# A decoder trunk on one core: the third place for a weight sum, and a held load

## The chip, the cores and the metric

The kernel runs on one core of a Trainium2 chip. The metric is the device time of one execution in microseconds; the time before is the median of three runs.

The engines are TensorE (PE: matmuls, and PEld for the loads of their stationary operand), VectorE (DVE), ScalarE (ACT), GpSimd (POOL) and SyncE (SP). Each runs its own list of instructions in order and waits on semaphores for the others. SP, ACT and POOL also issue DMA transfers; an issue stands in its engine's list like any instruction.

## The reference

Two layers, each of a mixing sublayer and a SwiGLU feed-forward sublayer, with a residual and a layer norm behind each. x is 512 tokens by 1024 channels in float32. The mixing sublayer starts with one projection of x, cut into the operands of two branches, attention and retention:

```python
z = jnp.einsum('bsd,dc->bsc', x, w_in) + b_in
q_a, k_a, v_a, q_r, k_r, v_r, g_r, gate_a, gate_b = jnp.split(z, SPLIT_POINTS, axis=-1)
for gi, (window, dilation) in enumerate(ATTN_GROUPS):      # (128, 1), (512, 4), (2048, 16)
    o, lse = _dilated_window_attention(q_a[:, :, gi], k_a[:, :, gi], v_a[:, :, gi], bias, window, dilation)
    ...
wts = jax.nn.softmax(jnp.stack(lses, axis=0), axis=0)
y_a = jnp.sum(wts[..., None] * jnp.stack(outs, axis=0), axis=0)
y_r = _retention(q_r, k_r, v_r)                            # 4 heads, chunkwise
merged = sigmoid(gate_a) * (y_a @ w_attn_proj) + sigmoid(gate_b) * (silu(g_r) * y_r) @ w_ret_proj
x = layer_norm(ALPHA * x + merged @ w_out);  x = layer_norm(ALPHA * x + swiglu(x))
```

Attention has six heads of width 64 in each of three groups. Query t of a group looks at the keys t, t - d, ..., t - window, with a bias by distance. The groups' outputs are added with weights that come from the softmax denominators.

## The kernel before

**Precision.** Every float32 matmul is three matmuls: each operand is split into a high part (a cast on ScalarE, `whi`, `xh`) and a low part (a subtraction on VectorE, `wlo`, `xl`), and high by high, high by low and low by high are added up in PSUM.

**Products.** Most projections are done with seven half-size products in place of eight (a Strassen-Winograd scheme). The weights of such a group are four blocks B11, B12, B21 and B22 and sums of them: P1 = B11 + B12, P2 = P1 + B22, P3 = B12 + B22, P4 = P2 + B21. Sums of x (`xs`) are made once per layer. The products are numbered 1 to 7 and add up in three PSUM accumulators A, X and C: products 1, 6, 7 and 4 in A, 2 in X, 5 and 3 in C. `ORDER` lists them with their operands, and two other orders are cut from it:

```python
ORDER = ((1, "A11", "B11"), (2, "A12", "B21"), (5, "S1", "P1"), (3, "S4", "B22"),
         (6, "S2", "P2"), (7, "S3", "P3"), (4, "A22", "P4"))
WIDE = tuple(ORDER[i] for i in (0, 2, 4, 1, 5, 3, 6))     # products 1, 5, 6, 2, 7, 3, 4
WIDE1 = tuple(ORDER[i] for i in (0, 1, 2, 4, 3, 5, 6))    # products 1, 2, 5, 6, 3, 7, 4
```

`wide` runs a group on TensorE: per product, 2 column halves by 4 slices of the contraction by 3 matmuls. After each product `ev` reads its accumulator (L810 a copy on ScalarE, L812, L815 and L818 sums on VectorE), and the next product in the same accumulator waits for that reading. `Right` makes the weight operands: it loads blocks into `raw` buffers (a pool of eight, each 128 x 1024), makes the sums on VectorE (L374 for P1 and P3, L378 for P2 and P4), and the high and low parts (L356 on ScalarE, L362 on VectorE).

**The attention stage**, once per layer. First come projections of q and k for the first pair of heads, then of v (two groups of `tall`, whose sums at the end are L505 and L508, and which write v to memory). Then, for the second and third pair of heads, comes a third-order projection of q and k (L233, L95, L783) followed by `qk_group`, one group of `wide` for both other orders. These are four groups of `qk_group` in all, two per layer. While TensorE works on a pair's projections, the blocks of the pair before run as side work, cut into small steps: `scores` (two small matmuls per block into `px`, then L572 on VectorE and the exponentials L574 on ScalarE), `turn` (transposes L583 on TensorE, and the copy L584 into `sT`), `values` (matmuls of `sT` with v, and the copy L595). Behind a pair's blocks comes a tail that weighs the two orders of groups: it writes their maxima and denominators to memory (L609) and reads them back in another arrangement (L612 into `mb`), works out the weights (L618 to L628), writes the second order's weights (L627, `wb` to `exd2`), reads them back rearranged (L631 into `fa`), and then expands, transposes and applies them (L638 on POOL, L644 on TensorE, L649 to L653). The tails of the first two pairs run beside the next pair's blocks, the third beside the first retention head.

**What sets the order.** The code gives instructions in one order, and a scheduler reorders each engine's list by its own estimate of when operands are ready. So where an instruction stands in an engine's list is seen in the built program, not in the code. Once built, each engine's order is fixed. L609, L612, L627 and L631 are all issued on ScalarE.

Of the kernel before, what the change touches and what calls it, by code (L numbers as in the profile page):

```python
# [15 lines left out]
ALU = mybir.AluOpType  # L16
# [3 lines left out]
P = 128  # L20
# [3 lines left out]
NI = S // P  # L24
# [30 lines left out]
def hybrid_kernel(ctx, tc, x, rel_bias, w_in, b_in, w_attn_proj, w_ret_proj, w_out,  # L55
# [3 lines left out]
    pe, act, dve, pool = nc.tensor, nc.scalar, nc.vector, nc.gpsimd  # L59
# [25 lines left out]
    def mm3(ps, ah, al, bh, bl, start, stop):  # L85
        mm(ps, ah, bh, start, False)
        mm(ps, ah, bl, False, False)
        mm(ps, al, bh, False, stop)

    def psum(name="px"):  # L90
        return psm.tile([P, S], F32, tag="mm", name=name)
# [5 lines left out]
    def raw(name="raw"):  # L97
        return rawp.tile([P, 1024], F32, tag="raw", name=name)

    def work(name):  # L100
        return wk.tile([P, S], F32, tag="w2", name=name)
# [4 lines left out]
    def view(t, a, b):  # L106
        return t[:, :a * b].rearrange("p (a b) -> p a b", a=a)

    def load(src, a, b):
        v = view(raw(), a, b)  # L110
        for v_, s_ in pieces(v, src):
            nc.sync.dma_start(v_, s_)
        return v
# [211 lines left out]
    WIDE = tuple(ORDER[i] for i in (0, 2, 4, 1, 5, 3, 6))  # L325
    WIDE1 = tuple(ORDER[i] for i in (0, 1, 2, 4, 3, 5, 6))

    class Right:
# [8 lines left out]
        def load(self, *names):  # L337
            for n in names:
                if (n, 0) in self.t:
                    continue  # L340
                for u, (a, b) in enumerate(self.shapes):
                    if n == "P1" and not self.adds:
                        self.t[n, u] = view(raw(), a, b)
                        continue
                    r = self.t[n, u] = load(self.src({"P1": "B11", "P3": "B12"}.get(n, n), u), a, b)
                    if n in ("P1", "P3"):
                        pool.dma_start(r, self.src({"P1": "B12", "P3": "B22"}[n], u), accum_op=ALU.add)  # L347
# [18 lines left out]
        def begin(self, n):  # L366

            if n == "B11":
                self.load(*self.loads)
            elif n in ("P1", "P3") and not self.adds:  # L370
                for u in range(len(self.shapes)):
                    if n == "P3":
                        self.t[n, u] = self.t["B12", u]
                    dve.tensor_tensor(out=self.t[n, u], in0=self.t["B12", u], in1=self.t["B11" if n == "P1" else "B22", u], op=ALU.add)  # L374
            elif n in ("P2", "P4"):
                for u in range(len(self.shapes)):
                    r = self.t["P1", u]
                    dve.tensor_tensor(out=r, in0=r, in1=self.t["B22" if n == "P2" else "B21", u], op=ALU.add)  # L378
            return self.high(n)
# [57 lines left out]
    def wide(right, left, ev):  # L437


        ps = {}  # L440
        for (i, an, bn), ((h, l),) in zip(right.order, right.operands()):
            c = CHAIN[i]
            if i in FIRST:
                ps[c] = psum("ps")
            for q in range(2):
                cs = slice(q * P, (q + 1) * P)
                for k in range(4):
                    ah, al = left(an, k, slice(0, 256))
                    mm3(ps[c][:, q * 256:(q + 1) * 256], h[:, k, cs], l[:, k, cs], ah, al,
                        i in FIRST and q == 0 and k == 0, k == 3)  # L450
                    tick(STEP / 2)
            ev(i, ps[c])
# [91 lines left out]
    def toeplitz(h, off, n):  # L544
        return bass.AP(tensor=bflat.tensor, offset=bflat.offset + h * (L0 + 2 * L1) + off + P - 1,
                       ap=[[HPG * (L0 + 2 * L1) - 1, P], [1, n]])

    def attention_pair(hp, qk, v, yp, bias, yaT):


# [26 lines left out]
        def turn(i, od):  # L577
            pxs, s, j0 = wrk[i, od]
            sT = wk.tile([P, 2, 2 * P], F32, tag="w2", name="sT")
            px = pxs[0].rearrange("p (h c) -> p h c", h=2)  # L580
            for hh in range(2):
                for j in range(j0, 2):
                    pe.transpose(px[:, hh, j * P:(j + 1) * P], s[:, hh, j * P:(j + 1) * P], ident)  # L583
            act.copy(out=sT[:, :, j0 * P:], in_=px[:, :, j0 * P:])  # L584
            wrk[i, od] = (pxs, sT, j0)

        def values(i, od):
# [9 lines left out]
        fa = sm.tile([P, 2, NI, 2], F32, tag="fa", name="fa", bufs=2)  # L597
# [30 lines left out]
            dve.tensor_tensor(out=fa[:, 0], in0=ea[:, 0], in1=wa, op=ALU.mult)  # L628

        def weighed():  # L630
            act.dma_start(fa[:, 1], exd2.rearrange("(l r) c -> l r c", r=4))  # L631

        wide_, weights = {}, {}
# [52 lines left out]
    def layer(ly, cp):  # L686
# [80 lines left out]
        with stage("attn") as ap_, stage("attw", 4) as aw:  # L767
# [17 lines left out]
            def qk_group(hp):  # L785

                def src(b, u):
                    k = 4 if b[1] == "2" else 0
                    c = (C_KA if b[2] == "2" else C_QA) + hp * P
                    return w_l[:, k:k + 4, c:c + 2 * GW].rearrange("p k (g c) -> p k g c", g=2)[:, :, :, :P]  # L790

                sn = {}

                def put(v, j, half):
                    for g in range(2):
                        bs = (bQs[ly], bT)[j]
                        c = (0, C_KA // P)[j] + (g * GW + hp * P) // P
                        o_, i_ = qk[hp, g][:, j], v[:, g]
                        if g:
                            o_ = o_.rearrange("p (r l) -> p r l", r=4)[:, :, half * 64:half * 64 + 64]  # L800
                            i_ = i_.rearrange("p (l r) -> p r l", r=4)
                        else:
                            o_ = o_[:, half * 256:half * 256 + 256]
                        act.activation(out=o_, in_=i_, func=AF.Identity, bias=bs[:, c:c + 1], scale=(HD ** -0.5, 1.0)[j])

                def ev(i, ps):
                    p2 = ps.rearrange("p (q t) -> p q t", q=2)
                    if i in (1, 5, 6):
                        sn[i] = view(work("sn"), 2, 256)
                        act.copy(out=sn[i], in_=p2)  # L810
                    elif i == 2:
                        dve.tensor_tensor(out=sn[1], in0=p2, in1=sn[1], op=ALU.add)  # L812
                        put(sn[1], 0, 0)
                    elif i == 3:
                        dve.tensor_tensor(out=sn[6], in0=p2, in1=sn[6], op=ALU.subtract)  # L815
                        put(sn[6], 1, 0)
                    elif i == 7:
                        dve.tensor_tensor(out=sn[5], in0=sn[5], in1=p2, op=ALU.subtract)  # L818
                        put(sn[5], 1, 1)
                    elif i == 4:  # L820
                        put(p2, 0, 1)

                wide(Right(src, [(4, 256)], WIDE, ("B11", "B12", "P1", "B22", "B21"), False), x_left, ev)

            if ly == 0:
                x0 = [slot("x0", F32) for _ in range(NI)]
# [154 lines left out]
            n = [nothing]  # L981
# [8 lines left out]
        with stage("ret") as rp:  # L990
# [139 lines left out]
            for dp in range(KD // 2):  # L1130
                h, l = was[dp]
# [239 lines left out]
```

## Time and profile before

| | |
|---|---|
| median of 3 runs | 2170.4 us (2165.8 to 2170.66) |
| the profiled execution | 2161.78 us, its span 2160.0 us |
| TensorE busy | 2134.5 us of the span |
| VectorE, ScalarE busy | 1475.8 us, 1046.5 us |
| data moved by DMA | 351.30 MB, 163 GB/s mean |

The profile shows one execution. A row of a timeline gives the start in us from the span's start, the length, the engine, the line of the kernel, the operation and its tiles (out<-in), how many instructions are merged into the row, and in brackets how long the engine idled before it and what ended that. `ACTq` and `SPq` are the issuing of DMAs by ScalarE and SyncE; the data move later.

### The profile page before, as it was taken

The page shows a single profiled execution, that of the slowest core. Times are in us where ns is not written, and L with a number is a line of the kernel's source. Part 1 is how long each engine was busy: PE and PEld are TensorE (multiplying, and loading weights), DVE is VectorE, ACT ScalarE, POOL GpSimd, SP SyncE. Part 2 cuts the span into 40 slices and gives each one's busy share as a digit, 9 for nine tenths or more (in the row PEclk, how much of TensorE's full clock was granted, in tenths as well). Part 3 has the DMA queues.
Part 4 walks back from the last instruction along what each step waited for, and adds up shares of the span by engine and source line. Part 5 has one row for each costly group of instructions (what it writes and reads, how often), then busy time and mean ns, then how long its engine had stood idle before and what let it go on. Part 6 is the DMA issues. An engine that isn't in the chain of part 4 may idle for free.

```text
span 2160.0 us, 34404 instructions
## 1 busy us (share of the span) xinstructions
PE 2134.5 (99%) x13770; PEld 1913.0 (89%) x13770; DVE 1475.8 (68%) x2101; ACT 1046.5 (48%) x1631; POOL 239.7 (11%) x249
## 2 busy tenths in 40 slices
PE   9999999999999999999999999999999999999998
PEld 8878888889988899989898888888899889999996
DVE  6645897887744675747676568887867357666575
ACT  4456655655723253525245665555666234444350
POOL 5010111011000100000020111111010001010001
PEclk9999999999999999999999999999999999999999
DMA  9944558577786366566268454667777662666551
GB/s 251 242 112 102 128 147 211 150 183 176 216 278 198 75 166 139 166 136 156 89 164 222 115 144 118 152 175 188 177 185 247 232 195 59 181 142 172 122 156 40
DMA packets 317634, 351.30 MB, mean 163 GB/s; under 512 B 22174, under 2 KB 255810, under 8 KB 317345
## 3 DMA queue, kind: packets, MB, share of 16 engines
q1 hardware_dynamic: 231936, 253.01, 38.6%
q0 software_dynamic: 58256, 83.29, 20.9%
q10 hardware_dynamic: 27280, 12.80, 2.1%
q8 instruction: 108, 1.77, 0.3%
q14 instruction: 54, 0.43, 0.1%
HBM read 323.26 MB, written 28.53 MB: 163 GB/s over the span
## 4 chain that ended last, share of the span: by engine, by line
PE 91%; issue 4%; DMA 2%; DVE 1%; ACT 1%; POOL 1%; SPq 0%; POOLq 0%; ACTq 0%; DVEq 0%
PE ps L83 82%; PE px L83 7%; PE px L583 1%; DMA exd<-wb 1%; DMA raw<-in_w_in 1%; PE px L1036 1%; PE px L192 0%; POOL ry L134 0%; DMA mb<-exd 0%; ACT whi L356 0%; DVE xtok L1166 0%; PE px L644 0%; DVE wlo L362 0%; DMA raw<-in_w_ffn_gate 0%; DMA v_d<-sn 0%
## 5 line engine op out<-in xcount | busy, mean ns | idle before, releaser
L362 DVE TENSOR_TENSOR wlo<-raw,whi 128x1024 fp32r<-128x1024 f32 (+1 forms) x448 | 521.8, 1167 | 268.7 <-ACT whi L356 261.3
L356 ACT CAST whi<-raw 128x1024 fp32r<-128x1024 f32 (+1 forms) x448 | 447.4, 1001 | 468.6 <-PE ps L83 266.5
L83 PE MATMUL ps<-xs,whi 128*128 128x256 f32 (+1 forms) x2816 | 552.2, 295 | 0.0
L83 PEld LDWEIGHTS ps<-xs,whi 128*128 128x128 f32 x2816 | 447.1, 191 | 18.2 <-issue 5.1
L83 PE MATMUL ps<-xh,whi 128*128 128x256 f32 (+1 forms) x1440 | 438.2, 306 | 1.7 <-ACT xh L94 1.4
L83 PE MATMUL ps<-xh,wlo 128*128 128x256 f32 (+1 forms) x1440 | 430.1, 300 | 1.0 <-DVE wlo L95 1.0
L83 PE MATMUL ps<-xl,whi 128*128 128x256 f32 (+1 forms) x1440 | 431.1, 300 | 0.0
L83 PE MATMUL ps<-xs,wlo 128*128 128x256 f32 (+1 forms) x1408 | 411.7, 292 | 0.0
L83 PEld LDWEIGHTS ps<-xh,whi 128*128 128x128 f32 x1440 | 273.9, 191 | 21.8 <-issue 7.2
L83 PEld LDWEIGHTS ps<-xl,whi 128*128 128x128 f32 x1440 | 275.3, 191 | 10.1 <-DVE xl L95 0.6
L83 PEld LDWEIGHTS ps<-xh,wlo 128*128 128x128 f32 x1440 | 274.7, 191 | 10.1 <-DVE wlo L95 1.2
L83 PEld LDWEIGHTS ps<-xs,wlo 128*128 128x128 f32 x1408 | 269.3, 191 | 5.0
L95 DVE TENSOR_TENSOR wlo<-raw,whi 128x1024 fp32r<-128x1024 f32 (+2 forms) x116 | 134.9, 1166 | 162.9 <-ACT whi L94 162.8
L83 PE MATMUL ps<-whi,xs 128*128 128x512 f32 (+1 forms) x768 | 225.0, 362 | 0.9 <-ACT sn L501 0.9
L94 ACT CAST whi<-raw 128x1024 fp32r<-128x1024 f32 (+2 forms) x116 | 115.9, 1003 | 213.2 <-PE ps L83 140.1
L83 PE MATMUL ps<-whi,ht 128*128 128x512 f32 x576 | 178.3, 389 | 0.0
L347 POOL DMA_DIRECT2D raw<-in_w_in x80 | 99.4, 1249 | 603.3 <-DMA raw<-in_w_in 274.0
L83 PEld LDWEIGHTS ps<-whi,xs 128*128 128x128 f32 x768 | 137.8, 188 | 20.4 <-ACT sn L501 1.2
L378 DVE TENSOR_TENSOR raw<-raw 128x1024 f32<-128x1024 f32 (+1 forms) x128 | 148.9, 1163 | 7.9 <-DMA raw<-in_w_in 5.7
L83 PE MATMUL ps<-wlo,xs 128*128 128x512 f32 (+1 forms) x384 | 138.2, 360 | 0.1
L83 PEld LDWEIGHTS ps<-whi,ht 128*128 128x128 f32 x576 | 108.1, 188 | 22.3
L347 POOL DMA_DIRECT2D raw<-in_w_ffn_gate x40 | 51.8, 1294 | 682.9 <-DMA raw<-in_w_ffn_up 187.9
(206 smaller groups left out, 2906.9 us busy)
## 6 DMA issues: line engine op xcount, KB each, us to landing
raw<-in_w_in SPq DMA_DIRECT2D x160, 512.0 KB, 4.8
raw<-in_w_in POOLq DMA_DIRECT2D x64, 512.0 KB, 8.7
raw<-in_w_ffn_up SPq DMA_DIRECT2D x64, 512.0 KB, 4.2
raw<-in_w_ffn_gate SPq DMA_DIRECT2D x44, 512.0 KB, 4.8
raw<-in_w_ffn_down SPq DMA_DIRECT2D x44, 512.0 KB, 4.2
raw<-in_w_ffn_gate POOLq DMA_DIRECT2D x40, 512.0 KB, 6.6
raw<-in_w_in SPq DMA_DIRECT2D x72, 256.0 KB, 4.9
raw<-in_w_ret_proj SPq DMA_DIRECT2D x32, 512.0 KB, 6.0
```

The source lines that it names most:

```text
L83: pe.matmul(ps, lhsT=a, rhs=b, start=start, stop=stop, skip_group_check=True)
L94: act.copy(out=hi, in_=src)
L95: dve.tensor_tensor(out=lo, in0=src, in1=hi.bitcast(F32), op=ALU.subtract)
L347: pool.dma_start(r, self.src({"P1": "B12", "P3": "B22"}[n], u), accum_op=ALU.add)
L356: act.copy(out=h, in_=src)
L362: dve.tensor_tensor(out=l, in0=src, in1=h.bitcast(F32), op=ALU.subtract)
L378: dve.tensor_tensor(out=r, in0=r, in1=self.t["B22" if n == "P2" else "B21", u], op=ALU.add)
L583: pe.transpose(px[:, hh, j * P:(j + 1) * P], s[:, hh, j * P:(j + 1) * P], ident)
L1036: pe.transpose(px[:, t * P:(t + 1) * P], ys[i][:, t * P:(t + 1) * P], ident)
```

## The change

It has two parts. `qk_group` takes the order `WIDE1` in place of `WIDE`: B21's product comes second and P1's third. P1 is no longer made in a raw buffer of its own but in B11's, once B11's high and low parts exist, so a group takes four raw buffers and not five, and the loads come in the order B11, B21, B12, B22. The second part puts a small copy ahead of the load L631: 8 columns of the transposed block `sT` that was made latest when this step was coded are copied into the place in `fa` that the load then overwrites. The copy's values are never used; the load has to come behind it.

```diff
@@ Right.load
-                    if n == "P1" and not self.adds:
-                        self.t[n, u] = view(raw(), a, b)
-                        continue
                     r = self.t[n, u] = load(self.src({"P1": "B11", "P3": "B12"}.get(n, n), u), a, b)
@@ Right.begin
             elif n in ("P1", "P3") and not self.adds:
+                a, b = ("B11", "B12") if n == "P1" else ("B12", "B22")
                 for u in range(len(self.shapes)):
-                    if n == "P3":
-                        self.t[n, u] = self.t["B12", u]
-                    dve.tensor_tensor(out=self.t[n, u], in0=self.t["B12", u], in1=self.t["B11" if n == "P1" else "B22", u], op=ALU.add)
+                    r = self.t[n, u] = self.t[a, u]
+                    dve.tensor_tensor(out=r, in0=r, in1=self.t[b, u], op=ALU.add)
@@ attention_pair, turn
             act.copy(out=sT[:, :, j0 * P:], in_=px[:, :, j0 * P:])
+            latest["sT"] = sT
@@ attention_pair, weighed
+            act.copy(out=fa[:, 1], in_=latest["sT"][:, 0, P:P + 2 * NI].rearrange("p (i h) -> p i h", i=NI))
             act.dma_start(fa[:, 1], exd2.rearrange("(l r) c -> l r c", r=4))
@@ qk_group
-                wide(Right(src, [(4, 256)], WIDE, ("B11", "B12", "P1", "B22", "B21"), False), x_left, ev)
+                wide(Right(src, [(4, 256)], WIDE1, ("B11", "B21", "B12", "B22"), False), x_left, ev)
```

Line numbers move with it. In the rows of the changed program below L362 is L359, L374 is L371, L505 and L508 are L502 and L505, L572, L574, L583 and L584 are each one lower, L631 is L633 with the new copy at L632, and L644, L810 and L818 are two higher.

The lists below are what the built programs hold. The first place is VectorE at the end of layer 0's v projection. Before:

```order
L505 TENSOR_TENSOR sn<-ps,sn 128x288
L362 TENSOR_TENSOR wlo<-raw,whi 128x576
L508 TENSOR_TENSOR sn<-sn,ps 128x288
L374 TENSOR_TENSOR raw<-raw 128x1024
L508 TENSOR_TENSOR sn<-sn,ps 128x288
L95 TENSOR_TENSOR wlo<-raw,whi 128x1024 x2
L374 TENSOR_TENSOR raw<-raw 128x1024
L362 TENSOR_TENSOR wlo<-raw,whi 128x1024 x2
```

And in the changed program:

```order
L502 TENSOR_TENSOR sn<-ps,sn 128x288
L359 TENSOR_TENSOR wlo<-raw,whi 128x576
L505 TENSOR_TENSOR sn<-sn,ps 128x288 x2
L95 TENSOR_TENSOR wlo<-raw,whi 128x1024 x2
L359 TENSOR_TENSOR wlo<-raw,whi 128x1024
L371 TENSOR_TENSOR raw<-raw 128x1024
L359 TENSOR_TENSOR wlo<-raw,whi 128x1024
L371 TENSOR_TENSOR raw<-raw 128x1024
```

The sum P1 stood between the two L508; it now stands behind both of them, behind both L95 and behind B11's low part. Layer 1 has the same.

The second place is ScalarE's list in the first tail, with the next pair's blocks around it. Before:

```order
L621 ACTIVATE ea<-ea 128x16
L627 DMA exd_1180<-wb 128x4x2
L574 ACTIVATE s,ls<-s,nm 128x128 x2
L631 DMA fa<-exd_1180 128x8
L574 ACTIVATE s,ls<-s,nm 128x256 x2
L584 COPY sT<-px 128x2x128
L356 CAST whi<-raw 128x1024
```

In the changed program L627 is followed by the two L573 and the copy L583 with no DMA between, and the load stands some twenty rows on:

```order
L627 DMA exd_1180<-wb 128x4x2
L573 ACTIVATE s,ls<-s,nm 128x128 x2
L573 ACTIVATE s,ls<-s,nm 128x256 x2
L583 COPY sT<-px 128x2x128
...
L583 COPY sT<-px 128x512
L812 COPY sn<-ps 128x512
L632 COPY fa<-sT 128x8
L353 CAST whi<-raw 128x1024
L633 DMA fa<-exd_1180 128x8
```

In the second tail the load moves likewise, behind a later block in the first retention head. In the third the copy stands ahead of L612 and the load keeps its place.

The third place is TensorE at the end of each layer's second `qk_group`, with buffer numbers. `ps_1825` before and `ps_1822` now are accumulator A. Before:

```order
L83 MATMUL ps_1891<-xs_81,whi_2041 128x256 x2
L83 MATMUL ps_1891<-xs_81,wlo_2042 128x256
L583 MATMUL px_2073<-ident_75,s_2079 128x128 x4
L83 MATMUL ps_1825<-xh_79,whi_2100 128x256
L83 MATMUL ps_1825<-xl_80,whi_2100 128x256
...
L83 MATMUL ps_1825<-xh_79,wlo_2101 128x256
L83 MATMUL px_2074<-sT_2138,v_1664 64x128 x4
```

And in the changed program:

```order
L83 MATMUL ps_1822<-xs_81,whi_2040 128x256 x2
L83 MATMUL ps_1822<-xs_81,wlo_2041 128x256
L582 MATMUL px_2072<-ident_75,s_2078 128x128 x4
L646 MATMUL px_2178<-ident_75,fe_2153 128x128
L83 MATMUL px_2073<-sT_2137,v_1663 64x128
L83 MATMUL ps_1822<-xh_79,whi_2099 128x256
L83 MATMUL ps_1822<-xl_80,whi_2099 128x256
```

Product 4 now follows product 7 in the same accumulator. One of the four matmuls on the block `sT` just transposed, and one of the four weight transposes L644, have moved ahead of product 4; the block's other three stay 18 matmuls later. Products 2 and 5 to 7 change places in all four groups as the new order says.

More of the change, by code (lines that the diff above doesn't have):

```diff
@@ L546, in toeplitz @@
                        ap=[[HPG * (L0 + 2 * L1) - 1, P], [1, n]])
+    latest = {}
     def attention_pair(hp, qk, v, yp, bias, yaT):
```

## The prediction

> **What bounds the kernel now.** I read the page's busy times and its chain first, then who TensorE waited for, then the timelines of single engines at those waits.
>
> ```profile
> PE 2134.5 (99%) x13770; PEld 1913.0 (89%) x13770; DVE 1475.8 (68%) x2101; ACT 1046.5 (48%) x1631; POOL 239.7 (11%) x249
> PE 91%; issue 4%; DMA 2%; DVE 1%; ACT 1%; POOL 1%; SPq 0%; POOLq 0%; ACTq 0%; DVEq 0%
> PE ps L83 <- DVE sn L508: 5.5, 2, 2.8
> PE px L83 <- ACT sT L584: 3.8, 2, 2.8
> PE px L583 <- ACT s L574: 0.7, 1, 0.7
> ```
>
> TensorE is busy for 2134.5 of 2160.0 us, so only 25.5 us of idle time are there to be had, beside slow clock. The last three rows (engine, tile and line, whom it waited for: total us, times, longest) hold 10.0 us of it, and all three lie in the attention stage. Other work on VectorE or ScalarE that ends earlier or later buys nothing.
>
> The first wait comes at the end of the v projection, once per layer (the number in brackets is the idle time before the row, and what ended it):
>
> ```profile
> 92.64 0.29 PE L83 MATMUL ps<-whi,xs 128*128 128x288 f32 x1
> 94.25 0.29 PE L83 MATMUL ps<-whi,xl 128*128 128x288 f32 x1
> 95.60 1.22 DVE L374 TENSOR_TENSOR raw<-raw 128x1024 f32<-128x1024 f32 x1 [3.70 <-DMA raw<-in_w_in]
> 96.75 0.45 DVE L508 TENSOR_TENSOR sn<-sn,ps 128x288 f32<-128x288 f32 x1
> 97.25 0.40 PE L83 MATMUL ps<-whi,xh 128*128 128x288 f32 x1 [2.71 <-DVE sn L508]
> 1169.03 0.40 PE L83 MATMUL ps<-whi,xh 128*128 128x288 f32 x1 [2.77 <-DVE sn L508]
> ```
>
> The second L508 could start when the xs matmuls ended (92.64 + 0.29). It stands behind L374, the early sum P1 for the next group of products, which idled 3.70 us for its weights. So TensorE waits for a weight that only a later group of products reads.
>
> The other two waits come from ScalarE's queue, in the softmax weights of one head pair while the next pair's blocks run:
>
> ```profile
> 153.66 0.38 ACTq L627 DMA_DIRECT2D exd<-wb  x1
> 155.09 0.42 DVE L572 CUSTOM_DVE_ANT_0 s<-px,bias 128x256 f32<-128x256 f32 x1
> 159.07 0.34 ACTq L631 DMA_DIRECT2D fa<-exd  x1
> 159.46 0.51 ACT L574 ACTIVATE s<-s,nm 128x256 f32<-128x256 f32 x1 [4.50 <-DMA exd<-wb]
> 160.86 0.69 PE L83 MATMUL px<-sT,v 128*64 128x128 f32 x4 [2.81 <-ACT sT L584]
> 211.71 0.44 PE L583 MATMUL px<-ident,s 128*128 128x128 f32 x2 [0.74 <-ACT s L574]
> 1230.85 0.44 PE L83 MATMUL px<-sT,v 128*64 128x128 f32 x4 [1.01 <-ACT sT L584]
> ```
>
> The load L631 waits at the head of ScalarE's queue until the write L627 has landed, and the exponentials (L574) queue behind it although their scores were done at 155.5. By the counts above (two and one for four tails) layer 1's second pair has no TensorE gap. One gap leaves a slow clock behind (columns: stretch, length, PE busy, granted clock, DMA):
>
> ```profile
> 162.00:164.00 2.00, 2.00 (x8) 0.50 0.00 0
> 164.00:166.00 2.00, 2.00 (x16) 0.97 0.00 0
> 97.00:99.00 2.00, 1.75 (x13) 1.00 1.03 322
> ```
>
> Half clock from 160.86 to about 164.05 is 3.2 us at half speed, 1.6 us lost; I take 1.5. [...]
>
> **The change, part by part.** *Sum third.* In the changed program VectorE does both L508 and both casts' remainders (L95) before it touches the sum, so the two gaps go: 2.71 + 2.77 = 5.48 us. What comes next must be there 2.7 us earlier:
>
> ```profile
> 92.18 2.00 ACT L94 CAST whi<-raw 128x1024 fp32r<-128x1024 f32 x2 [1.43 <-PE ps L83]
> 94.78 0.42 SPq L112 DMA_DIRECT2D raw<-in_w_in  x1
> DMA to landing us min/median/max: 4.5/4.5/4.5
> 104.05 0.28 DVE L572 CUSTOM_DVE_ANT_0 s<-px,bias 128x128 f32<-128x128 f32 x1
> ```
>
> The casts end at 94.18, so two L95, 1.2 us each like L374 of the same size, end by 95.8. TensorE has twelve matmuls of product 4 left behind the gap, 0.134 us apart as the twelve from 92.64 to 94.25, so without the gap it asks for them at 94.54 + 1.6 = 96.1. The group's last weight lands at 94.78 + 4.5 = 99.3, and VectorE, after three more operations of 1.2 us, comes to the sum that reads it at 99.5 or later. The first scores are wanted 2.7 us before 104.05. So I price the next wait at 0; if the loads were late by the whole advance, 5.48 us would come back.
>
> *New neighbours on TensorE.* With this order products 7 and 4 follow each other in one accumulator, and 4 must wait until 7 has been read (L818). In each layer's first group eight small attention matmuls stand between and cover it. In the second group four transposes and one weight transpose stand there, then one matmul on the block just transposed:
>
> ```profile
> 193.29 0.39 PE L583 MATMUL px<-ident,s 128*128 128x128 f32 x2
> 193.65 0.36 PE L83 MATMUL ps<-xh,whi 128*128 128x256 f32 x1
> 193.93 0.59 ACT L584 COPY sT<-px 128x512 f32<-128x512 f32 x1 [1.07 <-PE px L583]
> 190.76 0.34 ACTq L609 DMA_DIRECT2D exd<-pk  x1
> DMA to landing us min/median/max: 1.4/1.4/2.3
> ```
>
> Before, 18 matmuls of product 4 hid the copy sT. Now TensorE has 0.13 us of other work until 193.93 + 0.59: it idles about 0.7 us, twice, 1.4 us lost. Bounds: 0 if the copy starts sooner, 2 x 2.8 if the write of L609, for which L612 waits just ahead of that copy, took 5.4 us as L627 did (153.66 to 159.07) and not 1.4.
>
> *One buffer less.* The group takes four raw buffers, not five, so the first retention head's loads on SP's queue move up one buffer, and POOL adds its P1 ahead of the next pair's bias loads:
>
> ```profile
> 140.19 1.41 POOL L347 DMA_DIRECT2D raw<-in_w_in  x1
> 142.11 0.38 ACTq L612 DMA_DIRECT2D mb<-exd  x1
> 150.24 0.17 DVE L618 TENSOR_TENSOR mn<-nm,mb 128x8 f32<-128x8 f32 x1 [6.96 <-DMA mb<-exd]
> ```
>
> The scores that read this bias come just ahead of the row at 155.09, so 1.4 us more in front of its loads, today done by 140.19, cost nothing. The load mb took 8.1 us because these big transfers ran beside it; that they now run earlier can only bring it in sooner. Value 0, bounds 0 to a gain below 1.
>
> *The hold.* It adds six small copies, priced by L607 of the same size at 0.2 us, on an engine that is 48% busy: 0. The load L631 now stands after a later block: in the first tail one cast (1.05 us) behind the third L810 of the group, about 182 in today's times, in the second behind the block whose sT is made at 232.40.
>
> ```profile
> 137.81 0.20 ACT L607 COPY pk<-nm 128x8 f32<-128x8 f32 x1
> 180.19 0.59 ACT L810 COPY sn<-ps 128x512 f32<-128x512 f32 x1
> 232.40 0.60 ACT L584 COPY sT<-px 128x512 f32<-128x512 f32 x1
> DMA to landing us min/median/max: 2.3/5.0/8.0
> 190.65 0.62 POOL L638 COPY fe<-fa 128x512 f32<-128x512 f32 x1 [22.77 <-ACT qk L804]
> 237.84 0.62 POOL L638 COPY fe<-fa 128x512 f32<-128x512 f32 x1 [15.56 <-PE px L583]
> 245.16 0.60 PE L644 MATMUL px<-ident,fe 128*128 128x128 f32 x4
> ```
>
> Landing is 2.3 to 8.0 us after issue: at most 190 and 241. The reader L638 starts at 190.65 for other reasons in the first tail; in the second it ends by 241.9 at worst, and TensorE uses it at 245.16. So nothing is late, the write has long landed when ScalarE comes to the load, and the three gaps go: 2.81 + 1.01 + 0.74 = 4.56 us, and the slow clock's 1.5. In the third tail the copy runs before the weights are made and the order stays; that wait costs TensorE nothing today.
>
> Sum: 5.48 + 4.56 + 1.5 - 1.4 = 10.1 us gained. The profiled execution took 2161.78 us (span 2160.0), so it would take about 2151.7; the median of the runs shown is 8.6 above it at 2170.4, so I forecast 2160.3 there.
>
> **Rivals.** *The first gap only moves:* loads fill this stretch, 322 GB/s in the row at 97, and TensorE, 2.7 us ahead, meets a load later. For it: that rate. Against it: no TensorE wait for a load among the rows of waits above, and the loads in place as worked out. Gain 10.1 - 5.5 = 4.6, time 2165.8. *The hold only moves the wait:* fa lands late, POOL's expansion and then TensorE's weight transpose (one of which now stands just ahead of product 4) wait as long as ScalarE did. Gain 5.5 - 1.4 = 4.1, time 2166.3. *Slower:* at the end of each second group the write of L609 lands as late as mb did, 8.1 us and not 1.4; ScalarE stands at L612, the copy sT behind it, and TensorE idles 6.7 us more, with 1.5 of slow clock each time: 10.1 - 2 x 8.2 = 6.3 lost, 2176.7. It decides above a landing of about 5 us. Against it: 1.4 to 2.3 in six of six, in a quiet stretch. *The hold does nothing* (the copy done at once, as in the third tail) has the hold rival's price, 2166.3; the listed order speaks against it.
>
> **Chances.** Forecast 0.68; gap moves 0.13; hold rivals together 0.12; slower 0.05; the rest, 0.02, no change. A change of 0.3% (6.5 us) is about what a measurement of this kernel can tell from none. The forecast is faster; the two middle cases, 4.6 and 4.1 us, are within 0.3%. I put 0.70 faster, 0.25 same, 0.05 slower (a few of the middle cases keep part of the other gap). The range reaches from 2153 (no new wait, runs as low as the lowest shown, 2165.8 - 12) to 2168 (the middle cases with 2 us of scatter).
>
> **What would show it.** Right: no TensorE wait for L508; L508 twice in a row; no ScalarE idle of over 4 us at the first two L631; clock 1.00 in the first tail; a wait of about 0.7 us for sT just ahead of each second group's product 4. Wrong: a TensorE wait on the first product's weights after 96 us, or on L638 or L644; ScalarE idle at L612.

## The result, and the profile after

The changed kernel takes 2151.1 us in the median of six executions (2149.38 to 2155.11), beside 2169.4 us (2165.5 to 2170.66) for the kernel before in the same comparison: a ratio of 0.9921, with a 95% interval of 0.9908 to 0.9934. That is 18.3 us, or 0.8%, faster. I had forecast 2160.3 us with a range of 2153 to 2168: the direction was right, the gain was put too low, and the time lies 1.9 us below the range. One execution recorded further down, of the kernel of experiment 7, took 3002.41 us at a mean clock of 0.648 and is left out of its median and ratio.

The profiled execution tells another story than the median. It took 2150.84 us with a span of 2149.1, 10.9 us less than the span of before (2160.0), and my sum was 10.1. So the sum holds between the two profiles, and what is missing lies between before's profiled execution (2161.78 us) and its other ones.

The page's busy times and one of TensorE's waits in the changed kernel (engine, tile and line, whom it waited for: total us, times, longest):

```profile
PE 2133.7 (99%) x13770; PEld 1912.7 (89%) x13770; DVE 1477.5 (69%) x2101; ACT 1048.6 (49%) x1637; POOL 237.6 (11%) x249
PE px L83 <- ACT sT L583: 1.1, 2, 0.6
```

TensorE's idle time went from 25.5 to 15.4 us. The waits for L508 (5.5 us), for sT at the load (3.8) and for s (0.7) are gone. Two waits for sT of 0.57 us are new, at the places that the prediction named:

```profile
186.33 0.43 PE L83 MATMUL px<-sT,v 128*64 128x128 f32 x2 [0.57 <-ACT sT L583]
1251.87 0.43 PE L83 MATMUL px<-sT,v 128*64 128x128 f32 x2 [0.57 <-ACT sT L583]
```

At the first place, VectorE's timeline in layer 0 has both subtractions in a row, then the casts' remainders, and the sum last:

```profile
90.45 0.45 DVE L505 TENSOR_TENSOR sn<-sn,ps 128x288 f32<-128x288 f32 x1
91.98 0.46 DVE L505 TENSOR_TENSOR sn<-sn,ps 128x288 f32<-128x288 f32 x1 [1.07 <-PE ps L83]
92.35 2.35 DVE L95 TENSOR_TENSOR wlo<-raw,whi 128x1024 fp32r<-128x1024 f32 x2
97.13 1.23 DVE L371 TENSOR_TENSOR raw<-raw 128x1024 f32<-128x1024 f32 x1 [0.45 <-DMA raw<-in_w_in]
```

The sum still waits for its weights, now for 0.45 us, and nobody waits behind it.

In the first tail something happened that I had put at nothing. These are rows of the timelines of ScalarE and VectorE in the changed kernel, and then the stretch of 140 to 150 us, first in the changed kernel and then in the kernel before (the last three columns are the granted clock, the DMA engines' share and GB/s):

```profile
139.08 0.38 ACTq L612 DMA_DIRECT2D mb<-exd  x1
143.66 0.17 DVE L618 TENSOR_TENSOR mn<-nm,mb 128x8 f32<-128x8 f32 x1 [1.83 <-DMA mb<-exd]
146.07 0.37 ACTq L627 DMA_DIRECT2D exd<-wb  x1
172.61 0.34 ACTq L633 DMA_DIRECT2D fa<-exd  x1
```

```profile
140.00:150.00 10.00, 10.00 (x55) 7.70 (x53) 5.37 (x17) 3.04 (x9) 1.32 (x1) 1.00 0.64 118
```

```profile
140.00:150.00 10.00, 10.00 (x72) 8.66 (x72) 3.05 (x3) 5.47 (x11) 1.59 (x2) 1.00 0.95 213
```

Before, mb was asked for at 142.11 and used at 150.24. Now it is asked for at 139.08 and used at 143.66: 4.6 us and not 8.1. The write L627 goes out at 146.07 and not at 153.66, and from 140 to 150 us the DMA engines' share is 0.64 where it was 0.95. The big loads run earlier: from 120 to 130 and from 130 to 140 us the DMA engines moved 161 and 201 GB/s, where they moved 75 and 154 before. That the buffer set free is the cause is tested in experiments 6, 9 and 10.

### The profile page after: what moved, and what is told of

It reads as the page before. It is cut to its first block, busy times and chain, and to the rows that moved or that the text cites. A ratio compares the mean times of both kernels' runs of the same rounds, so it can differ in the third digit from the quotient of the medians.

```text
span 2149.1 us, 34408 instructions
## 1 busy us (share of the span) xinstructions
PE 2133.7 (99%) x13770; PEld 1912.7 (89%) x13770; DVE 1477.5 (69%) x2101; ACT 1048.6 (49%) x1637; POOL 237.6 (11%) x249
## 4 chain that ended last, share of the span: by engine, by line
PE 93%; issue 4%; DVE 1%; DMA 1%; POOL 1%; ACT 0%; POOLq 0%; DVEq 0%; ACTq 0%
PE ps L83 84%; PE px L83 7%; PE px L582 1%; PE px L1038 1%; DMA raw<-in_w_in 1%; PE px L192 1%; POOL ry L134 0%; DMA raw<-in_w_ffn_gate 0%; DVE xtok L1168 0%; PE px L646 0%; DVE xtok L1177 0%; ACT xh L94 0%; DVE stats L1179 0%; DVE wlo L359 0%; ACT whi L353 0%
## 5 line engine op out<-in xcount | busy, mean ns | idle before, releaser
L359 DVE TENSOR_TENSOR wlo<-raw,whi 128x1024 fp32r<-128x1024 f32 (+1 forms) x448 | 521.4, 1166 | 269.4 <-ACT whi L353 262.5
L83 PEld LDWEIGHTS ps<-xl,whi 128*128 128x128 f32 x1440 | 275.0, 191 | 10.1 <-DVE xl L95 0.6
L83 PEld LDWEIGHTS ps<-xh,wlo 128*128 128x128 f32 x1440 | 274.6, 191 | 10.1 <-DVE wlo L95 1.2
L95 DVE TENSOR_TENSOR wlo<-raw,whi 128x1024 fp32r<-128x1024 f32 (+2 forms) x116 | 135.0, 1167 | 163.8 <-ACT whi L94 163.6
L375 DVE TENSOR_TENSOR raw<-raw 128x1024 f32<-128x1024 f32 (+1 forms) x128 | 149.5, 1168 | 6.8 <-DMA raw<-in_w_in 4.5
```

Of the source, the lines that this page charges most:

```text
L83: pe.matmul(ps, lhsT=a, rhs=b, start=start, stop=stop, skip_group_check=True)
L95: dve.tensor_tensor(out=lo, in0=src, in1=hi.bitcast(F32), op=ALU.subtract)
L359: dve.tensor_tensor(out=l, in0=src, in1=h.bitcast(F32), op=ALU.subtract)
```

## Experiments

All ratios are to the kernel before in the same session, with 95% intervals.

### 1. The kernel before again, three traces

No edit. The first of these was also timed; the other two are single executions in later sessions.

> The kernel before, unchanged, to see how its executions differ. The changed kernel's profiled execution is 10.9 us shorter in span than before's (2149.1 against 2160.0), close to my sum of 10.1, but its median is 18.3 us lower. So before's profiled execution was an uncommonly short one. Theory A (some wait of before is longer in most executions than in the profiled one): this profile has a span near 2168 and shows, at one or more of the three places (VectorE's second L508, L631 of the first or the second tail), gaps of TensorE that are together some 4 to 8 us longer, or more stretches at clock 0.50. Theory B (the time between profiled and timed executions has nothing to do with the three waits): the three gaps are as before, 2.7 to 2.8 us, and the rest of the time shows elsewhere. Ratio to before 1.000 under both.

> One more profiled execution of the kernel before. For each of its three gaps of over 2 us: if the windows of 3.413 us are counted from any slow stretch of this execution, a gap that covers 2.2 us or more of one window is followed by a window at clock 0.50, a gap that covers 1.7 us or less of every window it touches is not. Without such a grid, slow clock follows the longest gaps alone.

> The kernel before once more, for its trace. The windows of 3.413 us counted from one slow stretch of this execution put every other slow stretch on a multiple, and a gap is followed by slow clock where it covers 2.2 us or more of one window, and not where it covers 1.7 us or less of each.

The first took 2164.15 us, ratio 0.9999 (0.9989 to 1.0008). The single executions took 2162.1 and 2167.09 us. The first trace was again a short one (2163.14 us), with gaps of 2.54, 2.39 and 2.47 us. It shows no longer wait, and being short it does not decide between its two theories. The other two bear out a grid of 3.413 us, the length of the one slow stretch in the middle of before's first profile (160.70 to 164.11 us). TensorE's timeline of the longest one at its three gaps, and then its clock over stretches of 3.4 us (columns: stretch, length, PE busy, granted clock, DMA share, GB/s):

```profile
97.90 0.61 PE L83 MATMUL ps<-whi,xh 128*128 128x288 f32 x1 [3.73 <-DVE sn L508]
163.04 0.70 PE L83 MATMUL px<-sT,v 128*64 128x128 f32 x4 [2.91 <-ACT sT L584]
1172.15 0.40 PE L83 MATMUL ps<-whi,xh 128*128 128x288 f32 x1 [2.27 <-DVE sn L508]
```

```profile
94.30:97.70 3.40, 0.00 (x0) 1.00 0.84 241
97.70:101.10 3.40, 3.20 (x13) 0.50 1.05 323
159.20:162.60 3.40, 0.93 (x5) 1.00 0.29 33
162.60:166.00 3.40, 2.96 (x12) 0.50 0.01 1
166.00:169.40 3.40, 3.40 (x16) 0.50 0.00 0
169.40:172.80 3.40, 3.40 (x32) 1.00 0.25 56
1169.50:1172.90 3.40, 1.13 (x8) 1.00 1.15 329
1172.90:1176.30 3.40, 3.40 (x14) 0.50 1.13 350
```

Here all three gaps left slow clock, one of them for two stretches: four times 3.4 us at a granted clock of 0.50, in which TensorE was busy for 12.96 us, so about 6.5 us lost in all (an estimate: half of the 12.96). The stretches begin at 97.7, 162.6 and 1172.9 us; 64.9 and 1075.2 us are 19.0 and 315.0 times 3.413. So the slow stretches of this execution lie on one grid, and here each window at full clock in which TensorE was busy for 1.13 us or less was followed by one at half clock.

The other single execution has the counterexample. Its slow stretches begin at 96.9 and 161.8 us, 19.0 times 3.413 us apart as well. Its gap of 2.77 us in layer 1 left the clock at 1.00: the grid, counted from its slow stretch at 161.8, cut it in two. Its timeline at the gap, and the two windows of the grid and the next:

```profile
1169.89 0.40 PE L83 MATMUL ps<-whi,xh 128*128 128x288 f32 x1 [2.77 <-DVE sn L508]
```

```profile
1165.20:1168.60 3.40, 1.92 (x15) 1.00 1.22 294
1168.60:1172.00 3.40, 2.11 (x14) 1.00 1.11 346
1172.00:1175.40 3.40, 3.40 (x16) 1.00 0.92 267
```

A gap of 2.77 us cost nothing beyond itself, and one of 2.27 us in another execution, which fell into one window, cost about 1.7 us more (an estimate: half of the 3.40 us that TensorE was busy at 0.50 behind it). Length alone did not decide.

Over 70 executions of before in the sessions with the experiments, whose clock was recorded, time and mean clock go together (correlation -0.84): 2160.9 us at a mean clock of 0.998 (5 of them), 2163.1 at 0.997 (23), 2165.1 at 0.996 (29), 2167.3 at 0.995 (10), and 2167.4 to 2170.7 below (3). That is about 2.0 us per 0.001. The changed kernel's executions, in whose trace no slow window is found, have 0.9986 in the mean, and the trace of before with one has 0.998, those with two 0.997 and the one with four 0.995. (Each of these traces also ends at half clock, in before from 2154.1 us and in the changed kernel from 2144.2, so neither reaches 1.) A window of 3.41 us at half clock lowers the mean by 3.41 x 0.5 / 2160 = 0.0008 and, by estimate, costs 1.7 us, which is 2.2 us per 0.001. So before's scatter goes, for the most part, with the number of slow windows, by this estimate mostly two to five. The three gaps themselves stayed between 2.3 and 3.7 us in the four traces.

### 2. Only the order and the place of P1, no copy

```diff
             act.copy(out=sT[:, :, j0 * P:], in_=px[:, :, j0 * P:])
...
-            act.copy(out=fa[:, 1], in_=latest["sT"][:, 0, P:P + 2 * NI].rearrange("p (i h) -> p i h", i=NI))
             act.dma_start(fa[:, 1], exd2.rearrange("(l r) c -> l r c", r=4))
```

> Only the first part of the change (P1 third and in B11's place), the load L631 without the copy. By the two profiles it gains 5.5 us (the two L508 gaps) + 0.9 (a gap of 0.93 at 81.60 that is gone) - 1.1 (two new waits of 0.57 for sT): 5.3 us, ratio 0.9976. If the missing 7 us belong to the sum's wait for its weights, 12 us, ratio 0.9945. If they belong to ScalarE's wait for the written weights, it gains 5.3 or less and keeps the scatter of before.

It took 2155.09 us, ratio 0.9953 (0.9939 to 0.9966): 8.7 us below before (2163.75), more than the 5.3 of the two profiles. ScalarE idles even longer for the written weights (6.00 us, where it was 4.50), but earlier:

```profile
144.58 0.17 DVE L618 TENSOR_TENSOR mn<-nm,mb 128x8 f32<-128x8 f32 x1 [1.69 <-DMA mb<-exd]
146.98 0.37 ACTq L627 DMA_DIRECT2D exd<-wb  x1
150.88 0.34 ACTq L632 DMA_DIRECT2D fa<-exd  x1
151.27 0.40 ACT L573 ACTIVATE s<-s,nm 128x128 f32<-128x128 f32 x1 [6.00 <-DMA exd<-wb]
```

ScalarE idled for 6.00 us and TensorE has no gap there: this wait falls while TensorE still has matmuls of the group. So the first part of the change takes away the gap of 2.8 us that I had credited to the copy. At two other tails, layer 0's second and layer 1's first, gaps of 0.53 and 0.67 us remain.

### 3. Only the copy

The products in the old order, P1 in a buffer of its own, the copy ahead of L631.

```diff
+            act.copy(out=fa[:, 1], in_=latest["sT"][:, 0, P:P + 2 * NI].rearrange("p (i h) -> p i h", i=NI))
             act.dma_start(fa[:, 1], exd2.rearrange("(l r) c -> l r c", r=4))
```

> Only the second part (the copy ahead of L631), products in the old order. By the two profiles it gains 2.81 + 1.01 + 0.75 + 1.5 of slow clock = 6.1 us, ratio 0.9972. If the missing 7 us belong to ScalarE's wait for the written weights, 13 us, ratio 0.994. If they belong to the sum's wait, 6 us or less, with the scatter of before, and the profile shows TensorE waits for L508 of 2.7 us or more, perhaps with slow clock behind them.

It took 2156.07 us, ratio 0.9958 (0.9945 to 0.9970), 7.7 us below before. The gaps of the tails are gone and those of L508 remain, with slow clock behind both in the trace (0.50 from 97.2 to 100.6 us behind the first). The timelines of TensorE and VectorE at the first, and the clock around the second:

```profile
96.76 0.40 PE L83 MATMUL ps<-whi,xh 128*128 128x288 f32 x1 [3.56 <-DVE sn L508]
95.12 1.23 DVE L374 TENSOR_TENSOR raw<-raw 128x1024 f32<-128x1024 f32 x1 [4.55 <-DMA raw<-in_w_in]
```

```profile
1162.20:1165.60 3.40, 1.17 (x9) 1.00 1.14 337
1165.60:1169.00 3.40, 3.40 (x12) 0.50 1.08 337
```

TensorE came to the first gap at 93.20, about a microsecond earlier than in three of the four traces of before, and waited that much longer: the gap's end is set by the landing of the sum's weights.

Alone, the parts gain 8.7 and 7.7 us, 16.4 together, while the whole change gains 12.9 (next experiment). The first tail's gap and its slow clock are in both.

### 4. The changed kernel again

> The changed kernel, unchanged, beside before in one session with the other runs. Before's median was 2169.4 us where the change was first timed and 2163.8 beside the experiments. Theory A (the changed kernel is steady, before is not, since each of its three gaps of 2.4 to 2.8 us leaves or does not leave 1.7 us of slow clock, as the phase of a grid of 3.41 us falls, and its waits for weights vary): the changed kernel is at 2150 to 2152 again, ratio 0.990 to 0.995 as before's own level falls, with no TensorE stretch at clock 0.50 between 30 and 2140 us. Theory B (the first comparison was an accident of the session): the changed kernel moves with before, ratio 0.992 within 0.001.

It took 2151.42 us (2150.91 to 2153.75), ratio 0.9944 (0.9931 to 0.9957): 12.9 us below before, which was at 2164.33 beside it. As theory A had it, the changed kernel is where it was first, 0.3 us off, while before is 5 us lower than in the first comparison. In the trace no stretch between 30 and 2140 us has slow clock. Over the changed kernel's 11 executions the mean clock is 0.9986, against 0.9962 over the 70 of before: 0.0024, or at 2.0 us per 0.001 about 4.8 us of the 12.9. This is an estimate from a correlation.

### 5. Old order of products, P1 in B11's place, with the copy

```diff
-                wide(Right(src, [(4, 256)], WIDE1, ("B11", "B21", "B12", "B22"), False), x_left, ev)
+                wide(Right(src, [(4, 256)], WIDE, ("B11", "B12", "B22", "B21"), False), x_left, ev)
```

> The change with one piece undone: the products keep the old order 1, 5, 6, 2, 7, 3, 4, but P1 is made in B11's place and loads come as B11, B12, B22, B21; the copy ahead of L631 stays. If being made in B11's place (and so behind B11's low part) is what lets L508 go first, the two gaps stay away as in the changed kernel; and products 7 and 4 are apart again, so the two waits of 0.57 us for sT go: 1.1 us below the changed kernel, about 2150.0, ratio 0.9916. If the third place in the order is what counts, the sum is needed one product earlier, TensorE meets a wait at the second product of about one product's length less what the sum is ahead (up to 2.7 us, twice), and the time is 2152 to 2156.

It took 2150.7 us, ratio 0.9933 (0.9919 to 0.9946). Its interval overlaps that of the changed kernel, which ran in another session, so the 1.1 us are not settled by the time. The trace shows no wait for L505 or L508 and none for sT; its two longest waits lie elsewhere:

```profile
PE ps L83 <- ACT xh L94: 2.3, 4, 1.5
PE ps L83 <- ACT sn L498: 1.9, 2, 1.5
```

So the third place in the order isn't needed to let the subtraction go first. P1 in B11's place has to wait for B11's low part, and that is enough.

### 6. P1 third, but in a buffer of its own, with the copy

```diff
+                    if n == "P1" and not self.adds:
+                        self.t[n, u] = view(raw(), a, b)
+                        continue
...
-                wide(Right(src, [(4, 256)], WIDE1, ("B11", "B21", "B12", "B22"), False), x_left, ev)
+                wide(Right(src, [(4, 256)], WIDE1, ("B11", "B21", "B12", "P1", "B22"), False), x_left, ev)
```

> The change with P1 in a raw buffer of its own again, third in order, loads B11, B21, B12, B22, the copy ahead of L631 kept. The sum then does not depend on B11's low part, and in the built list of VectorE it stands ahead of the second L508 again; its weights come one load later than before. Theory A (the place of the sum in VectorE's list is what TensorE waited for, and only making it in B11's place moves it): the gaps are back at both places and longer, 2.7 to 6 us each, with slow clock behind those that fill more than about 2 us of a window: 5 to 13 us above the changed kernel, 2156 to 2164. Theory B (third in order is enough): no such gap, and a time within 2 us of the changed kernel.

It took 2165.29 us, ratio 1.0007 (0.9998 to 1.0015): 13.9 us above the changed kernel in the same session, a little more than theory A allowed. The wait for the subtraction (here L509) is back and longer, and the first is followed by two slow windows. TensorE's waits, and its clock there:

```profile
PE ps L83 <- DVE sn L509: 9.6, 2, 4.9
```

```profile
92.90:96.30 3.40, 0.46 (x4) 1.00 1.15 319
96.30:99.70 3.40, 1.64 (x7) 0.50 1.05 318
99.70:103.10 3.40, 3.40 (x12) 0.50 0.66 183
```

The load mb took 8.2 us again, so the order of the loads does not bring it in sooner. Third in order without the shared buffer gains nothing, even with the copy.

### 7. The load issued by GpSimd in place of the copy

The changed order, no copy.

```diff
-            act.dma_start(fa[:, 1], exd2.rearrange("(l r) c -> l r c", r=4))
+            pool.dma_start(fa[:, 1], exd2.rearrange("(l r) c -> l r c", r=4))
```

> The changed order, without the copy, and the load L631 issued by GpSimd and not by ScalarE: the wait for the written weights then stands in GpSimd's list, whose next work, the expansion of these weights, needs them anyway. Theory A (the cost was that ScalarE's exponentials stood behind a DMA wait): as good as the copy, within 1.5 us of the changed kernel, no TensorE wait for s or sT but the two of 0.57 us. Theory B (someone has to wait, and GpSimd's weight loads behind it come late): TensorE waits for a whi or wlo of the first retention heads or of the second pair, 2 to 6 us, and the time is 2153 to 2158.

It took 2150.8 us in the median of five executions (2150.73 to 2154.04), ratio 0.9943 (0.9929 to 0.9958), beside 0.9944 for the changed kernel in the same session. TensorE waits for sT at the two known places and for no s:

```profile
PE px L83 <- ACT sT L583: 1.1, 2, 0.6
```

This is theory A: GpSimd, whose next work needs these weights, can wait at no cost that shows. The run tests it only on the gaps of 0.53 and 0.67 us that experiment 2 had left, since the first tail's gap was gone already.

### 8. Gaps filled with matmuls that nobody reads

Before, with 16 matmuls of 128x256 in each L508 gap.

```diff
+                if fill and i == 4 and a == 1:
+                    px = psum()
+                    for _ in range(fill):
+                        mm(px[:, :256], xh[:, 0, :P], xh[:, 0, :256], True, True)
                 for j, ((h, l), k) in enumerate(ks):
```

> The kernel before with 16 matmuls of 128x256 whose result nobody reads, in TensorE's list just ahead of the matmul that waits for the second L508, in both layers (about 1.9 us of work inside each gap of 2.5 to 2.8 us). The waits themselves stay, so nothing gets earlier. Theory A (the scatter of before is slow clock: a window of 3.41 us in which TensorE idled more than about 2 us is followed by one at half clock, 1.7 us lost): these two gaps can no longer leave slow clock; the mean granted clock rises by 0.0005 to 0.0015 over before's in the same session, and the median falls by 1 to 3.4 us, ratio 0.9985 to 0.9995, with no stretch at 0.50 behind 97 or 1167 us. Theory B (slow clock has another cause): the clock stays within 0.0003 of before's, ratio 0.9997 to 1.0010.

It took 2167.41 us, ratio 1.0011 (1.0001 to 1.0021), while its mean clock was 0.0007 above before's in that session (0.9964 against 0.9957). The clock did what theory A said, the time did not. The trace has the gaps filled but for 0.41 us in layer 0 and 1.18 us in layer 1, and slow clock behind neither (1.00 from 98 to 100 and from 1168 to 1170 us); it has it behind a gap of 2.58 us in layer 1's first tail, which was 0.6 to 1.4 us in the four traces of before. TensorE's timeline, and its clock behind that last gap:

```profile
95.67 2.07 PE L83 MATMUL px<-xh 128*128 128x256 f32 x16
98.15 0.40 PE L83 MATMUL ps<-whi,xh 128*128 128x288 f32 x1 [0.41 <-DVE sn L512]
1231.05 0.70 PE L83 MATMUL px<-sT,v 128*64 128x128 f32 x4 [2.58 <-ACT sT L588]
```

```profile
1227.40:1230.80 3.40, 1.07 (x5) 1.00 0.27 31
1230.80:1234.20 3.40, 3.15 (x12) 0.50 0.00 0
```

At equal mean clock this kernel is 3.4 us slower than before in the same session (at 0.996, 2168.2 against 2164.8). So it seems that the fillers cost waits of their own; why the later wait grew, this run does not tell. So no run shows a kernel that gets shorter by losing slow windows alone; that rests on the correlation of experiment 1.

### 9. Seven raw buffers

The kernel of experiment 2 with `rawp` at seven buffers.

```diff
-    rawp = ctx.enter_context(tc.tile_pool(name="rawp", bufs=8, side="right"))
+    rawp = ctx.enter_context(tc.tile_pool(name="rawp", bufs=7, side="right"))
```

> The changed order without the copy, as in the second experiment, but with seven raw buffers in the pool and not eight, so that the group's four stand to the pool about as five of eight did. In the second experiment the load mb landed in 4.3 us and the first tail's wait for L631 cost TensorE nothing, though ScalarE still idled 6.0 us. Theory A (the buffer set free is what moved the big loads out of mb's way): mb takes 7 to 8.5 us again, L627 is issued some 5 us later, and TensorE's gap of 2 to 3 us for sT in the first tail is back. Theory B (the order of the products moved it): mb lands in 4 to 5 us as before this edit. The whole time says nothing here, since later stages lose a buffer too.

One execution, 2167.91 us. The longest mb took 7.5 us, as theory A said, and L627 went out at 151.69, 4.7 us later than in experiment 2. But the write landed in 3.0 us, and TensorE's gap in the first tail is 0.57 us and not 2 to 3, against theory A. A gap of 2.91 us stands later, at a weight transpose that waited for GpSimd's expansion; GpSimd had idled 10.08 us there for a load of weights, so this gap looks like a cost of the missing buffer and not of mb. The landing of mb, and TensorE's timeline:

```profile
DMA to landing us min/median/max: 1.8/2.4/7.5
```

```profile
155.60 0.71 PE L582 MATMUL px<-ident,s 128*128 128x128 f32 x2 [0.57 <-ACT s L573]
224.66 0.66 PE L645 MATMUL px<-ident,fe 128*128 128x128 f32 x4 [2.91 <-POOL fe L639]
```

With experiment 6 this says that the buffer, and not the order, decides when mb lands. A late mb alone did not bring back TensorE's gap; the write landed in 3.0 us here and in 5.4 before, which may be why, but no run varied it alone.

### 10. P1 in B11's place alone

The kernel of experiment 2 with the old order of products: one edit to the kernel before, in effect.

```diff
-                wide(Right(src, [(4, 256)], WIDE1, ("B11", "B21", "B12", "B22"), False), x_left, ev)
+                wide(Right(src, [(4, 256)], WIDE, ("B11", "B12", "B22", "B21"), False), x_left, ev)
```

> The smallest piece: P1 made in B11's place, loads B11, B12, B22, B21, with the old order of products and without the copy. Theory A (this one edit carries the gain, by two ways: the sum can't run ahead of the second L508 any more, and the buffer set free moves the big loads out of the way of mb): no TensorE wait for L508, mb lands in 4 to 5 us, no gap over 1 us in the first tail of layer 0, mean clock 0.998 to 0.999, and a time 9 to 13 us below before, ratio 0.994 to 0.996. Theory B (the copy ahead of L631 is needed as well): gaps of 1 to 3 us for sT or s at L631 remain, with slow clock behind some, and the time is 5 to 8 us below before, ratio 0.9963 to 0.9977.

It took 2152.36 us, ratio 0.9943 (0.9930 to 0.9957), 12.7 us below before. The landing of mb, and TensorE's waits for sT and s:

```profile
DMA to landing us min/median/max: 1.9/2.1/3.0
```

```profile
PE px L83 <- ACT sT L583: 1.0, 2, 0.6
PE px L582 <- ACT s L573: 0.6, 1, 0.6
```

The old order with the buffer set free has mb early, as theory A said. This one edit has the ratio of the whole change. What the third place and the copy add to it is within the intervals.

## Why the prediction was right and wrong

*The two L508 gaps, 5.48 us.* Right: both are gone, and no later load took their place. The cause is narrower than I had it. Not the third place in the order moves the sum (experiment 6: third, and the gaps are 4.70 and 4.88 us), but the place in B11's buffer, which makes the sum depend on B11's low part (experiments 5 and 10: old order, no such gap).

*New neighbours on TensorE, 1.4 us lost.* Right in kind and place; 0.57 us twice, 1.1 us, where I had 0.7 twice.

*One buffer less, value 0, bounds 0 to a gain below 1.* Wrong, and the mechanism matters more than the time. I wrote that the big transfers would "only bring it in sooner" and left it there. mb landed in 4.6 us and not 8.1, the write L627 left 7.6 us earlier, and ScalarE's wait moved to where TensorE had other work (experiment 2). So the first part alone takes the first tail's gap. How much of that is mb's landing and how much the write's own (5.4 us before, 3.9 in experiment 2, and 3.0 in experiment 9, where mb was late and the gap stayed small) no run separates.

*The hold, 4.56 us and 1.5 of slow clock.* Right for what it does: in the first tail L633 is issued at 172.61, 26.5 us behind L627, and ScalarE does not wait. But with the first part in place only gaps of 0.53 and 0.67 us are left for it. I added the two parts as if they were independent; they share the first tail's 2.81 us and its slow clock. That the sum for the two profiles came out all the same (10.1 us, measured 10.9) is in part luck: the first tail's gap was counted once, if for the wrong part, and the profile of before had a wait of 0.93 us for L501 at 82.53, of which I had said nothing and which the changed kernel's profile does not have.

*Slow clock, 1.5 us, and the step to the median.* This is the step that failed: "the median of the runs shown is 8.6 above it at 2170.4, so I forecast 2160.3 there". I carried the offset of before over to the changed kernel, where it measured 0.3 us (2150.84 and 2151.1). The profiled execution of before had one slow window ahead of its end. The later executions mostly have two to five, by the recorded clocks: each of three gaps of 2.3 to 3.7 us may fall into one window of the grid, and one trace has a slow window at the start of the kernel as well (19.5 to 22.9 us). The changed kernel has no gap over 1 us in that stage and none of these windows in its traces. So the slow clock term, 1.5 us, should have been about 4.8 (by the correlation), and the offset of 8.6 should have been left out. In the later sessions before's median stands 2.0 to 3.6 us above its first profile of 2161.78; that much the slow windows can explain, and the rest of the 8.6 stays open, as said below. With 4.8 for the slow clock, and without the offset, the sum would be 5.5 + 4.6 + 4.8 - 1.1 = 13.8 us, beside 12.9 measured in the session of experiment 4.

The traces show that each of the three gaps could leave slow clock behind. In the longest trace of experiment 1 all three did: the slow stretches begin 19.0 and 315.0 times 3.413 us apart, and the gap of 2.27 us, which lay in one window, left 0.50 behind. My 1.5 us came from one gap in the rows of one execution, in which the gap of 2.71 us left the clock at 1.00.

*What stays open.* The first comparison gave 18.3 us and the later sessions 12.7 to 13.5 for the changed kernel and its equals. The difference is before's level, 2169.4 against 2163.8 to 2165.3. Executions of before at a mean clock of 0.995 or lower took 2166 us and more, so five to seven slow windows would fit (an estimate: four at 0.995, and 0.0008 for each more), but the clocks of those executions were not recorded. The later sessions ran on chips 13, 15 and 8, and the chip of the first comparison is not on record either, so a different chip is a rival. Neither is shown.

*The rivals.* The first gap did not move to a load. The hold did not move its wait to GpSimd or TensorE. The slower case needed a landing of L609 above 5 us at the end of the second groups. There L612 went out 1.9 us behind L609 (182.52 to 184.41, and 1248.06 to 1249.96), and the longest landing of L609 anywhere in the changed kernel's trace was 4.6.

## What to carry to other kernels

When a list is ordered by a scheduler, a buffer that is shared in place is an order: it makes the work wait for the last reader, and here that kept an early sum from standing in front of what TensorE needed. It frees a buffer as well, and earlier loads can move a small transfer that used to run beside them, as mb here (4.6 us and not 8.1). And a profile is one draw: where gaps can leave slow clock behind, as those of 2.27 to 3.73 us here, read the mean clock of several executions before carrying an offset between profile and median to a kernel that no longer has those gaps.

## What was unexpected of the hardware

Whether an idle gap left half clock behind went by a grid of 3.413 us in these traces. In before's first profile the clock is 0.50 from 160.70 to 164.11 us and then from 2154.08 us on, 584 times 3.413 us behind the first start. In the attention stage of the traces here, a window at full clock in which TensorE was busy for 1.17 us or less was followed by 3.4 us at 0.50 (the highest such is in experiment 3, from 1162.2 us), and one with 1.69 us or more was not (the lowest such is in the first trace of experiment 1, from 98.0 us). In these traces the bound lies between the two; no gap of chosen length was tried.

For a window already at half clock the busy time alone did not decide. In experiment 1's longest trace the one from 162.60 us, busy for 2.96 us, was followed by another (rows above). In experiment 6 one in layer 1 with nearly the same busy time was not:

```profile
1171.50:1174.90 3.40, 2.93 (x12) 0.50 0.50 149
1174.90:1178.30 3.40, 3.40 (x17) 1.00 0.75 227
```

The first of the two holds 0.70 us of matmuls of 128*64 (the row at 163.04); in the second the rows from 1171.97 to 1172.85 us are all of 128*128. What set the two windows apart, no run here tells.

One window at full clock lies outside the bounds above. In the first trace of experiment 1 a slow stretch stands at the start of the kernel, behind 3.4 us in which TensorE was busy for 2.83:

```profile
16.28 1.24 PE L83 MATMUL px<-hot,tab 33*6 33x383 f32 x4
```

```profile
16.10:19.50 3.40, 2.83 (x14) 1.00 1.12 321
19.50:22.90 3.40, 3.40 (x17) 0.50 0.66 177
```

1.24 us of it (the first row), and 0.59 more from 18.83 us, were matmuls of 33*6. Why half clock followed this window, no run here tells.
